# SSD units: the products of C with the states issued ahead of the multiplication that reads their PSUM bank

## The chip, the cores and the metric

The kernel runs on one core of a Trainium2 chip. The metric is the device time of one execution in microseconds (us), as the median of several runs. A core has five engines that run in parallel and meet only at semaphores: TensorE (PE, matrix products; its weight loads are shown apart as PEld), VectorE (DVE), ScalarE (ACT), GpSimd (POOL) and SyncE (SP, which here issues DMAs). Results of PE land in PSUM, which has banks of 512 float32 values for each of its 128 partitions.

## The reference, cut to what matters

One inference step of one layer of a hybrid decoder, in float32: 272 prompt rows (256 and 16 meta tokens) and 64 sample rows (8 sequences of 8 tokens), width 2048.

```
u = rmsnorm(h) @ w_in
h = h + concat[SSD(...), mLSTM(...)] @ w_out
h = h + (silu(gate) * val) @ w_down      # gate, val = split(conv(rmsnorm(h) @ w_up))
y = rmsnorm(h)
```

The change lies in the SSD part (Mamba-2, 32 heads in 2 groups, head width 64, state width 128). For each chunk of rows it computes

```
def step(S, inp):
    xc, dtc, Bc, Cc = inp
    cum = jnp.cumsum(dtc * Ag, axis=1)
    ...
    y = jnp.einsum('btsg,btsge,bsge,bsgep->btgep', CB, decay, dtc, xc)
    y = y + jnp.einsum('btgn,bgepn,btge->btgep', Cc, S, jnp.exp(cum))
    tail = jnp.exp(cum[:, -1:] - cum) * dtc
    S = S * jnp.exp(cum[:, -1])[..., None, None] + jnp.einsum('bsgn,bsge,bsgep->bgepn', Bc, tail, xc)
```

The second term of y is what matters here: the product of C with the state S, times exp(cum). The prompt has chunks of 16, 128 and 128 rows, so it needs C with two states (after 16 and after 144 rows). Each sample sequence has a carried state of its own.

## The kernel before, in words

Activations stand transposed: 128 features on the partitions, the rows in the free dimension (columns 0 to 255 prompt, 256 to 319 samples, then the meta tokens). The weights stream through in blocks of 128 x 1024 (8 tiles of 128 x 128) by DMA on SP's queue. Each weight block is split into a high and a low half of a shorter format (`hi` by ACT, `lo` by DVE), and each tile takes three matrix products (lines 203 to 205). The raw blocks and both halves have three buffers each, and the split runs two blocks ahead of PE.

The stages are: the input projection with the mLSTM heads, the input projection with the SSD units, the output projection, the up projection with a convolution, the down projection, and the final norm. In the SSD stage there are 16 units, each with two heads (128 features) and two projections (x and z) of 16 tiles each, so four weight blocks. A unit's own work is a Python generator (`unit`, line 781). `gemm` calls `tick` after each 8 tiles, and each tick lets every living generator take one step, up to its next `yield`. A unit's steps so spread over some two following units: convolution, decay matrices, transposes of xs (`transpose3`), E = exp(cum) (lines 828 to 830), the reads of the samples' states and the products within a chunk (lines 832 to 858), and the step of the change (lines 861 to 876). At one point of time PE therefore issues, after the last tile of one projection: unit j's step of the change, and right behind it unit j+1's transposes of xs (line 458), and then the next projection's tiles.

The step of the change works in one PSUM bank, `pe`, which the profile names nm after its tag (two banks of that tag):

- `turned` (line 483) transposes `ys`, the samples' reads of their states, into columns 256 to 383 of the bank (line 488);
- `es`, the 64 sample columns of E, is multiplied by it on DVE (line 863, the profile's line 72);
- two products on PE of C (`cf`) with the states S1 and S2 write columns 0 to 127 and 128 to 255 (lines 864 and 865);
- the prompt's 256 columns of E are multiplied by these on DVE (line 866);
- two state updates on PE (line 870) write two banks of the tag st, and DVE adds them to the states (line 872); E is added to y (line 873), POOL multiplies by the gate (line 874).

Two engines are kept from being in one PSUM bank at a time: where an instruction writes a bank, it waits for the earlier readers on other engines of any column of it. PE and SP issue in the order of the program (line 86); the order of DVE, ACT and POOL is chosen at build time by a planner with costs of its own, so a DVE instruction that is later in the program can come first if the planner expects its inputs sooner. Helpers record their own line in the profile: products line 69, DVE's two-operand operations line 72.

Of the kernel before, what the change touches and what calls it, by code (L numbers as in the profile page):

```python
# [13 lines left out]
ADD, SUB, MUL, MAX, MIN = ALU.add, ALU.subtract, ALU.mult, ALU.max, ALU.min  # L14
# [35 lines left out]
def hymba_kernel(ctx, tc, cst, xT, w0, w1, wo, wu, wd, shist, s0, c0n, fhist,  # L50
# [4 lines left out]
    def tl(pool, shape, dt=F32, tag=None, **kw):  # L55
        uid[0] += 1
        return pool.tile(shape, dt, tag=tag, name=f"{tag}_{uid[0]}", **kw)
# [10 lines left out]
    def mm(out, lhsT, rhs, start=True, stop=True):  # L68
        nc.tensor.matmul(out, lhsT, rhs, start=start, stop=stop)  # L69

    def tt(out, a, b, op):
        nc.vector.tensor_tensor(out, a, b, op=op)  # L72
# [10 lines left out]
    def bank(pool, n, tag="g"):  # L83
        return tl(pool, [P, 512], tag=tag)[:, :n]
# [6 lines left out]
    def C(name, i=0, n=None):  # L91
        o, w = _CST[name]
        return cs[:, o + i:o + (w if n is None else i + n)]
# [167 lines left out]
    a = []  # L261
# [26 lines left out]
    with ExitStack() as pa:  # L288
# [194 lines left out]
        def turned(ys, pst=None):  # L483

            n = ys.shape[1] // P
            pst = tl(pt, [P, 4, P], tag="tr") if pst is None else pst
            for i in range(n):
                nc.tensor.transpose(pst[:, i, :], ys[:, i * P:(i + 1) * P], C("ident"))
            v = pst[:, :n, :].rearrange("p i (b u t) -> p i u b t", u=4, t=TS)
            return [v[:, i, :2] for i in range(n)]  # L490
# [16 lines left out]
        def sb(t):  # L507
            return t.rearrange("p (s b t) -> p s b t", s=2, t=TS)
# [200 lines left out]
        with tc.tile_pool(name="sd", reuse_waits="tile", bufs=1) as sd:  # L709
# [71 lines left out]
            def unit(j, gc, pad, ps, zz):  # L781
# [50 lines left out]
                ys = tl(sd, [P, P], tag="ys")  # L832
# [27 lines left out]
                yield  # L860
                es = sb(E[:, NP:ND])
                pe = bank(pm, 512, "nm")
                tt(es, es, turned(ys, pe[:, 256:384].rearrange("p (a b) -> p a b", a=1))[0], MUL)
                mm(pe[:, 0:128], S1, cf[:, 0:128])
                mm(pe[:, 128:256], S2, cf[:, 128:256])
                tt(E[:, :256], E[:, :256], pe[:, :256], MUL)
                pps = [tl(pm, [P, 512], tag="st").rearrange("p (a b) -> p a b", a=4) for _ in range(2)]
                for i, pp in enumerate(pps):
                    rows = slice(32 * i, 32 * i + 32)
# [11 lines left out]
            for g in range(2):  # L881
                bc, gc = [], []
                pad = padded(16 + g)
                start(conv(pad, (early.pop(1 + g) if 1 + g in early else inproj(1 + g)), 16 + g, bc))
                pad = padded(18 + g)
                ps = (early.pop(3 + g) if 3 + g in early else inproj(3 + g))
                start(conv(pad, ps, 18 + g, bc, tl(sd, [P, T], tag="cf")))
                start(group(bc, gc))
                for j in range(8 * g, 8 * g + 8):
                    zz = []  # L890
                    pad = padded(j)
                    start(unit(j, gc, pad, (early.pop(5 + 2 * j) if 5 + 2 * j in early else inproj(5 + 2 * j)), zz))
                    start(zgate(inproj(6 + 2 * j, NQ), zz))
# [250 lines left out]
```

## Time and profile before

| | |
|---|---|
| median of 3 runs | 1961.93 us (1961.51 to 1962.8) |
| profiled execution | 1962.04 us |
| its span (first to last instruction) | 1960.3 us |
| granted TensorE clock, mean | 0.997 |
| PE busy | 1929.2 us (98%) |
| DVE busy | 1240.5 us (63%) |
| ACT busy | 856.3 us (44%) |
| POOL busy | 381.5 us (19%) |
| mean DMA rate | 163 GB/s |
| SSD units in the span | from about 455 to 800 us |

A line of the view in order of time has the start, the length, the engine, the line of the code, the operation, the tile written and the tiles read; xN says that N records were merged, and brackets hold the idle time of the engine ahead of it and what ended it. A line of the waits has the engine and tile that waited, for whom, the sum in us, the number of times and the longest. Ends of matrix products are modelled.

### The profile page before, as it was taken

How to read it: one execution, taken by the hardware profiler on the slowest of the kernel's cores; microseconds unless marked ns; L12 is line 12 of the kernel's file. 1: busy time of each engine (PE TensorE's matmuls, PEld its weight loads, DVE VectorE, ACT ScalarE, POOL GpSimd, SP SyncE). 2: the span in 40 equal slices, each digit the busy share in tenths (PEclk: the TensorE clock that was granted, in tenths of full speed). 3: DMA queues.
4: the chain of work that ended last, by engine and by line, in shares of the span. 5: the costliest groups of instructions: out<-in, count | busy, mean ns of one | idle time of the engine just before them, and what ended most of it. 6: DMA issues, size and time to landing. Idle time of an engine off the chain costs nothing.

```text
span 1960.3 us, 33606 instructions
## 1 busy us (share of the span) xinstructions
PE 1929.2 (98%) x13302; PEld 1891.2 (96%) x13302; DVE 1240.5 (63%) x2064; ACT 856.3 (44%) x1301; POOL 381.5 (19%) x721
## 2 busy tenths in 40 slices
PE   9999999999999999999999999999999999999997
PEld 8999999999989998999999999999999999999997
DVE  7877676777888788655547666655555556333344
ACT  6355555555444455433334444443334435333332
POOL 1211111212434343211112111111111110111111
PEclk9999999999999999999999999999999999999998
DMA  7545555546554655455554444444444444555553
GB/s 228 178 150 191 175 174 179 193 156 204 185 182 162 199 178 180 150 161 157 163 165 145 154 146 149 153 153 150 148 153 151 152 147 150 148 150 151 152 148 113
DMA packets 94221, 319.68 MB, mean 163 GB/s; under 512 B 10680, under 2 KB 19440, under 8 KB 92016
## 3 DMA queue, kind: packets, MB, share of 16 engines
q1 hardware_dynamic: 93744, 317.26, 50.7%
q8 instruction: 104, 1.70, 0.4%
q10 hardware_dynamic: 320, 0.28, 0.1%
q14 instruction: 53, 0.43, 0.1%
HBM read 294.80 MB, written 22.70 MB: 162 GB/s over the span
## 4 chain that ended last, share of the span: by engine, by line
PE 94%; DVE 3%; DMA 1%; issue 1%; ACT 1%; SPq 0%; DVEq 0%; ACTq 0%
PE g L69 87%; PE st L69 3%; PE nm L69 2%; DMA rowB<-scr_m 1%; PE tr L458 1%; DVE lo L72 1%; DVE blk L78 0%; DVE yb L72 0%; ACT hi L81 0%; DVE blk L72 0%; DMA raw<-in_w 0%; DVE co L78 0%; DVE pad L72 0%; DVE blk L552 0%; PE tr L69 0%
## 5 line engine op out<-in xcount | busy, mean ns | idle before, releaser
L69 PE MATMUL g<-blk,hi 128*128 128x322 f32 (+2 forms) x6240 | 1429.5, 313 | 0.0
L69 PEld LDWEIGHTS g<-blk,hi 128*128 128x128 f32 x6240 | 1054.1, 189 | 5.5 <-issue 4.8
L72 DVE TENSOR_TENSOR lo<-raw,hi 128x1024 fp32r<-128x1024 f32 (+3 forms) x509 | 652.6, 1282 | 464.6 <-ACT hi L81 459.5
L69 PE MATMUL g<-blk,lo 128*128 128x322 f32 (+2 forms) x2992 | 930.8, 311 | 0.0
L81 ACT ACTIVATE hi<-raw 128x1024 fp32r<-128x1024 f32 (+2 forms) x507 | 527.6, 1041 | 760.7 <-PE g L69 521.4
L69 PEld LDWEIGHTS g<-blk,lo 128*128 128x128 f32 x2992 | 563.8, 188 | 0.0
L69 PE MATMUL g<-ah,hi 128*128 128x322 f32 (+1 forms) x832 | 259.6, 312 | 0.0
L69 PE MATMUL g<-ah,lo 128*128 128x322 f32 (+1 forms) x832 | 259.5, 312 | 0.0
L69 PE MATMUL g<-al,hi 128*128 128x322 f32 (+1 forms) x832 | 258.8, 311 | 0.0
L69 PEld LDWEIGHTS g<-ah,hi 128*128 128x128 f32 x832 | 158.2, 190 | 0.1
L69 PEld LDWEIGHTS g<-al,hi 128*128 128x128 f32 x832 | 157.3, 189 | 0.1
L69 PEld LDWEIGHTS g<-ah,lo 128*128 128x128 f32 x832 | 157.1, 189 | 0.0
L72 DVE TENSOR_TENSOR fpad<-g,R 128x256 f32<-128x256 f32 (+2 forms) x264 | 54.6, 263 | 95.2 <-PE g L69 95.1
L235 POOL TENSOR_TENSOR blk<-h 128x322 f32<-128x322 f32 (+1 forms) x28 | 31.0, 1107 | 400.1 <-DVE h L72 231.8
L78 DVE SCALAR_TENSOR_TENSOR fcv<-fpad,fc,fcv 128x336 f32<-128x336 f32 x176 | 99.4, 567 | 3.9 <-ACT fcv L81 0.8
L976 POOL COPY fo<-fpad 128x2 f32<-128x2 f32 x88 | 17.5, 199 | 338.7 <-DVE fpad L72 338.6
L81 ACT ACTIVATE blk<-blk 128x322 fp32r<-128x322 f32 (+6 forms) x118 | 50.4, 450 | 51.7 <-DVE blk L78 20.9
L75 POOL TENSOR_TENSOR blk<-fsg,fcv 128x256 f32<-128x256 f32 x88 | 46.6, 553 | 112.2 <-PE g L69 60.9
L81 ACT ACTIVATE fcv<-fpad,fc 128x336 f32<-128x336 f32 x88 | 57.2, 652 | 0.1
L81 ACT ACTIVATE fsg<-fcv 128x336 f32<-128x336 f32 x44 | 21.3, 484 | 73.1 <-DVE fcv L78 73.1
L236 POOL TENSOR_TENSOR acc<-acc,blk 128x322 f32<-128x322 f32 (+2 forms) x46 | 51.8, 1126 | 2.5
L72 DVE TENSOR_TENSOR blk<-blk,blk 128x322 fp32r<-128x322 f32 (+3 forms) x76 | 38.9, 522 | 18.4 <-ACT blk L81 18.0
(212 smaller groups left out, 1340.0 us busy)
## 6 DMA issues: line engine op xcount, KB each, us to landing
raw<-in_wu SPq DMA_DIRECT2D x176, 512.0 KB, 3.7
raw<-in_w SPq DMA_DIRECT2D x164, 512.0 KB, 4.1
raw<-in_wd SPq DMA_DIRECT2D x80, 512.0 KB, 3.6
raw<-in_wo SPq DMA_DIRECT2D x64, 512.0 KB, 4.1
out_c_o<-co SPq DMA_DIRECT2D x8, 1156.5 KB, 7.4
out_ssd_o<-so SPq DMA_DIRECT2D x16, 576.0 KB, 3.7
C<-in_c0n SPq DMA_DIRECT2D x8, 1028.0 KB, 6.6
S<-in_s SPq DMA_DIRECT2D x16, 512.0 KB, 4.9
```

Source lines behind the costliest of these rows:

```text
L69: nc.tensor.matmul(out, lhsT, rhs, start=start, stop=stop)
L72: nc.vector.tensor_tensor(out, a, b, op=op)
L75: nc.gpsimd.tensor_tensor(out, a, b, op=op)
L78: nc.vector.scalar_tensor_tensor(out, a, s, b, op0=op0, op1=op1)
L81: nc.scalar.activation(out, a, f, **kw)
L235: eng.tensor_tensor(q, x, x, op=MUL)
L236: eng.tensor_tensor(self.acc[eng], self.acc[eng], q, op=ADD)
L458: nc.tensor.transpose(pst[:n, c, :], src[:, o:o + n], C("ident"))
L976: nc.gpsimd.tensor_copy(fo[:, li, 0:2], pad[:, 256:258])
```

## The change

The DVE multiplication of the samples' columns by the transposed reads is moved from between the transposes and the products of C with the states to behind the multiplication of the prompt's columns. Operands, tiles and banks stay as they are.

```diff
                 es = sb(E[:, NP:ND])
                 pe = bank(pm, 512, "nm")
-                tt(es, es, turned(ys, pe[:, 256:384].rearrange("p (a b) -> p a b", a=1))[0], MUL)
+                yt = turned(ys, pe[:, 256:384].rearrange("p (a b) -> p a b", a=1))[0]
                 mm(pe[:, 0:128], S1, cf[:, 0:128])
                 mm(pe[:, 128:256], S2, cf[:, 128:256])
                 tt(E[:, :256], E[:, :256], pe[:, :256], MUL)
+                tt(es, es, yt, MUL)
                 pps = [tl(pm, [P, 512], tag="st").rearrange("p (a b) -> p a b", a=4) for _ in range(2)]
```

## The prediction

> **What bounds the kernel now.** I read the totals of the page first, then the chain that ended last, then what TensorE (PE) waited for, then the order of time around the lines that the change touches.
>
> ```profile
> span 1960.3 us, 33606 instructions
> PE 1929.2 (98%) x13302; PEld 1891.2 (96%) x13302; DVE 1240.5 (63%) x2064; ACT 856.3 (44%) x1301; POOL 381.5 (19%) x721
> PE 94%; DVE 3%; DMA 1%; issue 1%; ACT 1%; SPq 0%; DVEq 0%; ACTq 0%
> ```
>
> PE is the bound: 1929.2 of 1960.3 us, and 94% of the chain. Nothing that other engines do counts unless PE stands for it. So the next view is the list of what PE waited for in the whole span, its four largest entries:
>
> ```profile
> PE nm L69 <- DVE pad L72: 9.0, 14, 0.7
> PE tr L458 <- DVE blk L72: 2.0, 3, 1.1
> PE nm L69 <- DVE lo L72: 1.7, 2, 1.1
> PE nm L69 <- DVE E L72: 1.5, 2, 1.1
> ```
>
> The columns are total us, times, longest. The first and the fourth are 14 + 2 = 16 waits, 10.5 us in all, one for each of the 16 SSD units: tile nm is written late because VectorE (DVE) has not finished with it. The view in order of time of one unit, and of the next one's start, shows what they are:
>
> ```profile
> 526.52 0.27 PE L488 MATMUL nm<-cs,ys 128*128 128x128 f32 x1
> 526.72 0.42 DVE L72 TENSOR_TENSOR pad<-g,R 128x256 f32<-128x256 f32 x1 [0.86 <-PE g L69]
> 527.06 0.21 DVE L72 TENSOR_TENSOR E<-E,nm 128x64 f32<-128x64 f32 x1
> 527.18 0.36 DVE L72 TENSOR_TENSOR pad<-g,R 128x64 f32<-128x64 f32 x3
> 527.41 0.68 PE L69 MATMUL nm<-cf,S 128*128 128x128 f32 x4 [0.63 <-DVE pad L72]
> 528.02 1.13 PE L69 MATMUL st<-xm,bt 32*128 32x512 f32 x4
> 529.08 0.55 PE L458 MATMUL tr<-cs,blk 128*128 128x128 f32 x3
> 529.39 0.54 PE L69 MATMUL g<-blk,hi 128*128 128x322 f32 x2
> 546.06 0.27 PE L488 MATMUL nm<-cs,ys 128*128 128x128 f32 x1
> ```
>
> At 526.52 PE transposes the samples' reads (line 863, through line 488) into columns 256 to 383 of bank pe. DVE is first busy with the 256-wide padding of the next unit (526.72), then multiplies E's 64 sample columns by the transposed reads (527.06 to 527.27). Only then, at 527.41, do the products of C with S1 and S2 begin (lines 864 and 865). They read none of what DVE made; they write columns 0 to 255 of the bank that DVE was reading. The trace puts the wait down to the padding, but the small padding at 527.18 feeds nothing in nm: the releaser is the E multiplication, whose end is 0.14 us ahead of the products.
>
> **The change part by part.** It removes, adds and resizes no instruction. On PE, whose order is the program's, the sequence stays transpose, two products (four records), two state updates, the next unit's transposes. What moves is one DVE instruction, the 64-wide multiplication (0.21 us), from ahead of the products to behind the 256-wide one. No DMA moves, so SP's and POOL's queues keep their order.
>
> *What goes.* The products no longer wait for DVE. From a transpose's start to the products' start:
>
> ```profile
> 487.35 0.27 PE L488 MATMUL nm<-cs,ys 128*128 128x128 f32 x1
> 488.31 0.68 PE L69 MATMUL nm<-cf,S 128*128 128x128 f32 x4 [0.69 <-DVE pad L72]
> 757.44 0.27 PE L488 MATMUL nm<-cs,ys 128*128 128x128 f32 x1
> 758.33 0.68 PE L69 MATMUL nm<-cf,S 128*128 128x128 f32 x4 [0.63 <-DVE pad L72]
> 776.72 0.27 PE L488 MATMUL nm<-cs,ys 128*128 128x128 f32 x1
> 778.08 0.68 PE L69 MATMUL nm<-cf,S 128*128 128x128 f32 x4 [1.08 <-DVE E L72]
> 796.49 0.27 PE L488 MATMUL nm<-cs,ys 128*128 128x128 f32 x1
> 797.17 0.68 PE L69 MATMUL nm<-cf,S 128*128 128x128 f32 x4 [0.41 <-DVE E L72]
> ```
>
> These are the first (0.96) and the fourteenth (0.89) of the ordinary units, and the last two (1.36, where DVE was behind with other work, and 0.68, where no padding stood ahead). Of the fourteen, three show 0.96, four 0.90 and seven 0.89: 2.88 + 3.60 + 6.23 = 12.71. With 1.36 and 0.68 the sixteen make 14.75 us.
>
> *What stays of it.* The transpose takes its own time in the stream, which the trace doesn't show in this place without a wait. Nearest rows: the three transposes at 529.08 are followed by g at 529.39, 0.31 / 3 = 0.10 us each; the four product records at 527.41 are followed by st at 528.02, 0.61 / 4 = 0.15 each. I take 0.15, since the products' weights have the products' own form and must be loaded in that step: 16 x 0.15 = 2.40. Saved: 14.75 - 2.40 = 12.35 us. With 0.10 it would be 13.15. The other end is the idle time that the trace itself charges, 10.5, which starts at the modelled end of the transpose's record (0.27 after its start). A record's length is not its place in a stream: at 529.08 three transposes fit into 0.31.
>
> The Trainium skill, in "TensorE: Matmul & The Clock Gate" (Single matmul latency and step 5, NX overlap), has a lone matmul last (398 + N) / 2.4 ns but successive ones start every N / 2.4: the drain lies under the next fill. For N = 128 that is 166 ns hidden; as an estimate from that page 16 x 0.166 = 2.7 on top of the idle time's 10.5 gives 13.2 saved. The transposes at 529.08 agree in kind: 0.10 apart, records 0.27 long.
>
> *The moved multiplication.* DVE now does the 64-wide one behind the 256-wide one. Its 0.21 us is the same work; the paddings come about 0.15 earlier for it. Behind it in program order stand the state additions, the addition to y and, through them, POOL's gating and ACT's E of the next unit. None of this is on the chain unless it makes PE wait later. So the question is what PE needs next, and how late it may come:
>
> ```profile
> 527.65 1.23 DVE L72 TENSOR_TENSOR lo<-raw,hi 128x1024 fp32r<-128x1024 f32 x1
> 530.85 0.61 DVE L813 TENSOR_TENSOR xp<-tr,colA 128x256 f32<-128x256 f32 x2
> 532.83 0.90 POOL L813 TENSOR_TENSOR xw<-xp,colA 128x256 f32<-128x256 f32 x1
> 534.18 1.76 DVE L72 TENSOR_TENSOR lo<-raw,hi 128x1024 fp32r<-128x1024 f32 x1
> 534.82 2.02 POOL L75 TENSOR_TENSOR xm<-xw,cs 64x512 f32<-64x512 f32 x1
> 538.26 0.61 PE L69 MATMUL st<-xw,bt 128*128 128x128 f32 x4
> 538.87 7.37 PE g L69 x48
> 540.81 0.46 DVE L78 SCALAR_TENSOR_TENSOR S<-S,dec,st 128x64 f32<-128x64 f32 x2
> 541.19 0.46 DVE L78 SCALAR_TENSOR_TENSOR so<-S,dec,st 128x64 f32<-128x64 f32 x2
> 541.58 0.70 DVE L78 SCALAR_TENSOR_TENSOR blk<-th,cv 128x256 f32<-128x256 f32 x4
> 546.96 0.68 PE L69 MATMUL nm<-cf,S 128*128 128x128 f32 x4 [0.63 <-DVE pad L72]
> ```
>
> (The row of 538.87 is from the chain.) The next products need S2, done at 541.27, and would start at 546.06 + 0.15 = 546.21: 4.9 us to spare. The state updates behind them need both "st" banks, the later one free at 541.65, against 546.82: 5.2 us. They also need xm, ready at 536.84. The transposes of the next xs need the four pieces of 541.58, done by 542.28, about 6 us before. The xw of 532.83 ends at 533.73; its first reader at 538.26 would come 0.74 earlier: 3.8 us. The weight halves run on a ring of three: the lo ending at 528.88 belongs to the block from 538.87 on, the one ending at 535.94 to the second half of that block, 3.7 later, more than 6 us ahead. All are larger than the 0.74 us that the unit becomes shorter, so no stall comes back in this place, and what PE gains in one unit it keeps.
>
> DVE's own load is the cover for all of these:
>
> ```profile
> 555.00:575.00 20.00, 19.38 (x147) 17.79 (x146) 16.80 (x33) 9.59 (x19) 8.74 (x11) 1.00 0.55 179
> ```
>
> Columns: length, busy us of PE, PEld, DVE, ACT, POOL, then granted clock, DMA share, GB/s. DVE is busy 84%. A unit is 546.06 - 526.52 = 19.54 us, of which DVE works 16.4; at 18.80 us it would be 87% busy, DMA 57% where it is 55% now. The clock is at 1.00 already and has nothing to give or to lose by 0.7 us less standing. From 798 us to the end PE waits once, so the shift reaches the end:
>
> ```profile
> PE g L69 <- DVE R L72: 0.2, 1, 0.2
> ```
>
> *The sum.* The profiled execution took 1962.04 us, its span 1960.3; the median of the runs is 1961.93, 0.11 lower. 1962.04 - 12.35 = 1949.7, and from the median 1949.6. That is 0.63% less; about 0.2% (3.9 us) is what a measurement of this kernel can tell from no change.
>
> **The rivals.**
>
> *The wait moves instead of going.* PE could meet its next DVE dependence, the "st" banks or the next xs, at the same point and stand as long. For: all the instructions behind the products depend on DVE work of the unit before. Against: the slack of 4.9 to 6 us worked out above. DVE would have to come some 5.5 us later than now. Time: 1961.9. Chance 4%.
>
> *Only part is kept.* DVE's order is chosen by a planner and not by the program, so the move can reshuffle paddings, lo halves and E's multiplications, and the last two units, where DVE is behind, can stand again. If the gain per unit fell to half, 16 x 0.37 = 5.9 saved: 1956. Chance 7%. Speaks against it: lo has over 6 us to spare.
>
> *Slower, by DVE standing at the head of its queue.* If the planner puts the 256-wide multiplication ahead of the paddings, DVE waits there for PE's products, 0.15 + 0.68 = 0.8 us after the last g, and with the state additions ahead too, 1.06 more. DVE then has 16.4 us of work and this standing in a unit of 18.80: up to 2.4 us it is free, beyond it each us lengthens the unit by one. The change would be a loss only from 19.54 - 16.4 = 3.1 us on; at 3.5 us the unit takes 19.9, 16 x 0.36 = 5.8 us more: 1967.7. The two items come to 1.9, below both points. Chance 5%.
>
> **How the numbers follow.** The likeliest case, the stall gone for good, has 84%; its own range runs from 13.15 saved (1948.8) to 10.5 saved (1951.4), and 0.8 wider at the low end, since the last two units and the rows' reading may give a little more. The whole range, 1948 to 1953, takes in the milder half of the partial case. Faster by over 0.2%: 84% and most of the partial case, 90%; within it 4% and a rest of 1%: 5%; slower 5%.
>
> **What would show it.** Right: the two entries of PE waiting for nm gone from the waits; from a transpose's start to the products' 0.10 to 0.15 us instead of 0.89; PE's busy time within a few us of 1929 and its idle time some 10 us less; a unit of about 18.8 us; the 64-wide E multiplication behind the 256-wide one on DVE. Wrong: a new entry of PE waiting for DVE at st, tr or g in this stage; products that start 0.3 us or more after the transposes; units shorter but a later stage longer because the planner ordered DVE, ACT or POOL differently there.

## The result and the profile after

The changed kernel takes 1948.09 us as the median of four runs (1947.21 to 1949.64), the kernel before, timed beside it, 1962.32 (1961.51 to 1962.8). The ratio is 0.9924, 95% interval 0.9911 to 0.9936: 0.76% faster, and a ratio so applied to the 1961.93 of before gives 1947.0. The direction and the mechanism were forecast; the size was 12.35 us and came out at 14 to 15.

The profiled execution took 1947.21 us, its span is 14.9 us shorter than that of before. First the page's lines, then PE's waits, its four largest entries (total us, times, longest):

```profile
span 1945.4 us, 33603 instructions
PE 1924.6 (99%) x13302; PEld 1890.9 (97%) x13302; DVE 1244.0 (64%) x2064; ACT 856.6 (44%) x1301; POOL 403.2 (21%) x721
```

```profile
PE nm L69 <- DVE lo L72: 2.2, 2, 1.6
PE tr L458 <- DVE blk L72: 1.7, 3, 0.8
PE g L69 <- POOL R L98: 1.2, 1, 1.2
PE nm L69 <- ACT hi L81: 0.9, 1, 0.9
```

The 9.0 and the 1.5 us for nm are gone; what is left is, in all but 0.2 us, from before 455 us, the start and the mLSTM stage. The busy times of the SSD stage, before and then after, say the same (columns: stretch, length, busy us of PE, PEld, DVE, ACT, POOL, granted clock, DMA share, GB/s): PE stood 10.47 us before and none after.

```profile
455.00:798.00 343.00, 332.53 (x2481) 307.80 (x2482) 286.12 (x566) 172.46 (x335) 135.07 (x165) 1.00 0.55 179
```

```profile
455.00:784.00 329.00, 329.00 (x2484) 308.20 (x2482) 289.66 (x569) 171.69 (x335) 154.16 (x168) 1.00 0.60 186
```

The order of time of the second unit of the changed kernel, PE and DVE:

```profile
506.70 0.27 PE L488 MATMUL nm<-cs,ys 128*128 128x128 f32 x1
506.80 0.61 PE L69 MATMUL nm<-cf,S 128*128 128x128 f32 x4
506.89 0.56 DVE L72 TENSOR_TENSOR pad<-g,R 128x256 f32<-128x256 f32 x2 [0.87 <-PE g L69]
507.34 1.13 PE L69 MATMUL st<-xm,bt 32*128 32x512 f32 x4
507.45 0.55 DVE L72 TENSOR_TENSOR E<-E,nm 128x256 f32<-128x256 f32 x2
508.04 0.49 DVE L72 TENSOR_TENSOR blk<-blk,E 128x320 f32<-128x320 f32 x1
508.40 0.55 PE L458 MATMUL tr<-cs,blk 128*128 128x128 f32 x3
508.56 1.29 DVE L72 TENSOR_TENSOR so<-S,st 128x512 f32<-128x512 f32 x2
510.57 1.21 DVE L72 TENSOR_TENSOR lo<-raw,hi 128x1024 fp32r<-128x1024 f32 x1
525.38 0.27 PE L488 MATMUL nm<-cs,ys 128*128 128x128 f32 x1
```

From transpose to products 0.10 us (0.89 before), from the products to the state updates 0.54 (0.61 before), a unit 525.38 - 506.70 = 18.68 (19.54 before). DVE's order changed more than the diff says: both multiplications of E now stand right behind two pieces of the padding, and the addition to y (`blk<-blk,E`) ahead of the lo half, which came first before.

### The profile page after: what moved, and what is told of

It is laid out like the page before. It is cut to its first block, busy times and chain, and to the rows that moved or that the text cites. A ratio compares the mean times of both kernels' runs of the same rounds, so it can differ in the third digit from the quotient of the medians.

```text
span 1945.4 us, 33603 instructions
## 1 busy us (share of the span) xinstructions
PE 1924.6 (99%) x13302; PEld 1890.9 (97%) x13302; DVE 1244.0 (64%) x2064; ACT 856.6 (44%) x1301; POOL 403.2 (21%) x721
## 4 chain that ended last, share of the span: by engine, by line
PE 95%; DVE 2%; DMA 2%; ACT 1%; issue 0%; SPq 0%; DVEq 0%; ACTq 0%
PE g L69 88%; PE st L69 3%; PE nm L69 2%; DMA rowB<-scr_m 1%; PE tr L458 1%; DVE lo L72 0%; DVE yb L72 0%; DMA raw<-in_w 0%; DVE co L78 0%; ACT hi L81 0%; ACT blk L81 0%; DVE blk L552 0%; PE tr L69 0%; DVE blk L72 0%; DVE Rs L1035 0%
## 5 line engine op out<-in xcount | busy, mean ns | idle before, releaser
L236 POOL TENSOR_TENSOR acc<-acc,blk 128x322 f32<-128x322 f32 (+2 forms) x46 | 70.1, 1524 | 3.5
```

The lines of the kernel that those rows point to most:

```text
L236: eng.tensor_tensor(self.acc[eng], self.acc[eng], q, op=ADD)
```

## The experiments

**The changed kernel again,** beside the three that follow.

> The changed kernel once more, timed beside the others. Theory (a whole stall per unit went: from the transpose's start to the state updates 1.50 us before, 0.64 after in an ordinary unit, 14.3 us over 16 units): 14.3 us less than before, between 13 and 15.5. Rival (the 14.9 us of the single comparison of spans hold more than the units, for instance a start or an up projection that runs faster in the changed kernel): 15 us or more again, with a part of it outside the units in the same place.

Measured: 1947.66 us (1946.42 to 1952.42) against 1962.55; ratio 0.9929 (0.9917 to 0.9942): 13.9 us less by the ratio, 14.9 by the medians, both within the forecast 13 to 15.5. Its profiled execution is the slowest of its runs, 1952.42 us, 5.2 slower than that of the first comparison. It shows where runs differ. Its first transpose of a unit is at 490.3 us and its last at 785.8, so the 15 steps take 295.5 us, and 783.51 - 488.02 = 295.49 in the first comparison. The units agree; the surplus lies ahead of them (2.3 us) and behind (2.9). Ahead, PE waits for DVE at the start of the program, and the clock granted right behind this wait is 0.50 for some 3 us. The wait is as long in the first comparison, 1.59 us in both, and there the clock stays at 1.00; the repeat has one more of 0.49 just ahead of it. The same stretch, in the repeat and then in the first comparison:

```profile
30.00:36.00 6.00, 4.14 (x15) 3.87 (x16) 5.28 (x8) 2.19 (x4) 0.00 (x0) 0.72 0.37 115
30.00:36.00 6.00, 4.33 (x27) 3.90 (x26) 5.26 (x7) 2.27 (x4) 0.00 (x0) 1.00 0.39 126
```

Behind, the up projection differs by itself. Its gate operation has 44 records; the line gives the start of the first and the last, in before and in the changed kernel:

```profile
L81 ACT ACTIVATE fsg<-fcv x44: 466/485/488, 1038.4 to 1632.2; 128x336 f32<-128x336 f32 x44
```

```profile
L81 ACT ACTIVATE fsg<-fcv x44: 463/484/487, 1024.7 to 1617.4; 128x336 f32<-128x336 f32 x44
```

From first to last 593.8 and 592.7, and 595.4 (1027.1 to 1622.5) in the repeat, with the same instructions. So the rival was partly right for the first pair of profiles: of 14.9 us, the units hold 14.3 (below), the start gave back 0.7, and 1.3 lie behind the units, 1.1 of it in the up projection. The start belongs to the run: the first transpose comes at 488.0 in one profile of this kernel and at 490.3 in the other. For the 1.1 this isn't shown. The three profiled kernels in which PE still waits (before, and two of the experiments below) all have 593.8 in the up projection, and those without the wait have 592.7 in five profiles and 595.4 in this repeat. So this part may go with the change by a way that no run shows, or with the run.

**The transposed reads in a bank of their own,** with the order of the program as before:

```diff
-                tt(es, es, turned(ys, pe[:, 256:384].rearrange("p (a b) -> p a b", a=1))[0], MUL)
+                tt(es, es, turned(ys)[0], MUL)
```

> The order of the program is that of before, but the transposed reads go to the bank of the tag tr instead of columns 256 to 383 of pe. Theory (PE stood because DVE read the bank that the products write): no wait of PE for nm, 0.10 us from the transpose to the products, and 14.3 us less than before (13 to 15.5), as with the change itself. Rival (the gain comes of the multiplication being late in DVE's order, with E's 256 columns ahead of it): the multiplication keeps its early place here, so little or nothing is gained, 0 to 4 us. A wait of PE for tr, where the next xs needs that one bank 1.7 us after the transpose, would show as an entry there; the multiplication ends some 0.75 us after it, so none is expected.

```profile
505.56 0.27 PE L488 MATMUL tr<-cs,ys 128*128 128x128 f32 x1
505.67 0.61 PE L69 MATMUL nm<-cf,S 128*128 128x128 f32 x4
506.10 0.21 DVE L72 TENSOR_TENSOR E<-E,tr 128x64 f32<-128x64 f32 x1
506.21 1.13 PE L69 MATMUL st<-xm,bt 32*128 32x512 f32 x4
```

Measured: 1945.9 us, ratio 0.9919 (0.9906 to 0.9933), as with the change. DVE's sample multiplication keeps its early place, 0.54 us after the transpose, and runs while PE multiplies. So what cost the time was the shared bank, and the multiplication's place on DVE is worth nothing by itself. The rival falls. PE's wait for tr, which could have taken the place, isn't there in this stage.

**Both products ahead of the transpose too,** against the changed kernel.

```diff
-                yt = turned(ys, pe[:, 256:384].rearrange("p (a b) -> p a b", a=1))[0]
                 mm(pe[:, 0:128], S1, cf[:, 0:128])
                 mm(pe[:, 128:256], S2, cf[:, 128:256])
+                yt = turned(ys, pe[:, 256:384].rearrange("p (a b) -> p a b", a=1))[0]
```

> As changed, but on PE both products stand ahead of the transpose too. Theory: PE streams the same records without a wait, so the same time as the changed kernel within 1 us (14.3 less than before). Rival (the transpose's place just behind the last projection tile is what makes it cheap, 0.10 us, or the products behind a transpose are cheap): per unit 0.05 to 0.15 us more, 1 to 2.4 us in all over the changed kernel.

```profile
505.29 0.60 PE L69 MATMUL nm<-cf,S 128*128 128x128 f32 x4
505.74 0.27 PE L488 MATMUL nm<-cs,ys 128*128 128x128 f32 x1
505.94 1.13 PE L69 MATMUL st<-xm,bt 32*128 32x512 f32 x4
```

Measured: 1947.52 us, ratio 0.9925 (0.9911 to 0.9938). From the first of the five records to the state updates 0.65 us, with the transpose first 0.64: the records cost the same in either order within 0.01 us, and the rival, 0.05 to 0.15, falls. The three kernels without the wait aren't told apart by their intervals, so none of them is better than the others.

**Half of the change:** one product ahead of the sample multiplication, one behind it (the diff is against the changed kernel).

```diff
                 mm(pe[:, 0:128], S1, cf[:, 0:128])
+                tt(es, es, yt, MUL)
                 mm(pe[:, 128:256], S2, cf[:, 128:256])
                 tt(E[:, :256], E[:, :256], pe[:, :256], MUL)
-                tt(es, es, yt, MUL)
```

> Half of the change: one product ahead of the sample multiplication, one behind it. Theory (the wait's length counts, and it ends when DVE is done): the first product (0.27 us) lies under the wait, DVE still ends some 0.75 us after the transpose's start, the second product starts at 0.89, its first record is 0.07 us longer as after any wait, and the state updates start at 1.23 instead of 1.50 before: 16 x 0.27 = 4.3 us less than before, 3 to 6. Rival (a wait costs a fixed restart whatever its length): one wait per unit remains, so nothing is gained, within 1 us of before. Rival 2 (what counts is DVE's order): the multiplication is early, nothing gained.

```profile
506.99 0.27 PE L488 MATMUL nm<-cs,ys 128*128 128x128 f32 x1
507.10 0.39 PE L69 MATMUL nm<-cf,S 128*128 128x128 f32 x2
507.53 0.21 DVE L72 TENSOR_TENSOR E<-E,nm 128x64 f32<-128x64 f32 x1
507.80 0.49 PE L69 MATMUL nm<-cf,S 128*128 128x128 f32 x2 [0.31 <-DVE E L72]
508.21 1.13 PE L69 MATMUL st<-xm,bt 32*128 32x512 f32 x4
```

Measured: 1958.9 us against 1962.55, ratio 0.9981 (0.9972 to 0.9989), 3.7 us less; forecast 4.3, 3 to 6. DVE is done at 507.74 and the second product begins 0.06 later: the wait ends with DVE, and the product put under it is free. Both rivals, which gave nothing, fall. The state updates start 1.22 us after the transpose, 1.23 forecast, but this hit is in part luck: the second product starts at 0.81 and not at 0.89, and takes 0.41 until the next instruction where 0.34 was forecast and half of 0.54 is 0.27. The fifteenth unit gains nothing: its updates start 2.15 after the transpose, 1.97 before.

**The wait lengthened,** in the kernel before; `dum` is a tile of its own that nothing reads, here and below.

```diff
-                tt(es, es, turned(ys, pe[:, 256:384].rearrange("p (a b) -> p a b", a=1))[0], MUL)
+                yt = turned(ys, pe[:, 256:384].rearrange("p (a b) -> p a b", a=1))[0]
+                tt(es, es, yt, MUL)
+                tt(sb(dum), sb(C("ones", 0, 64)), yt, MUL)
```

> The kernel before with the stall lengthened: DVE reads the transposed samples a second time (64 columns into a tile that nothing uses, some 0.2 us) right behind the multiplication and ahead of the products. Theory (PE stands exactly as long as DVE is in the bank): the products start 0.13 to 0.21 us later, 1.03 to 1.10 after the transpose's start, and the kernel is 16 x 0.13 to 0.21 = 2.1 to 3.4 us slower than before. Rival (a wait costs a fixed amount): same as before within 1 us.

```profile
527.89 0.27 PE L488 MATMUL nm<-cs,ys 128*128 128x128 f32 x1
528.92 0.68 PE L69 MATMUL nm<-cf,S 128*128 128x128 f32 x4 [0.76 <-DVE pad L72]
779.70 0.27 PE L488 MATMUL nm<-cs,ys 128*128 128x128 f32 x1
781.19 0.68 PE L69 MATMUL nm<-cf,S 128*128 128x128 f32 x4 [1.22 <-DVE dum L72]
```

Measured: 1964.62 us against 1962.54, ratio 1.0012 (1.0003 to 1.0021), 2.1 us more, at the lower edge of the 2.1 to 3.4. The interval is 0.6 to 4.1 us, so the time alone hardly shuts out the rival, which had at most 1 us. The trace does: the products start 1.03 after the transpose where it was 0.89, and over the sixteen units this wait makes 16.9 us, 14.75 before. PE stands as long as DVE is in the bank. The profiled run holds one thing more: in the fifteenth unit, where DVE is behind, the products start 1.49 after the transpose, and the granted clock falls right behind it:

```profile
779.00:785.00 6.00, 4.78 (x24) 3.63 (x23) 5.96 (x14) 2.52 (x5) 0.22 (x1) 0.82 0.51 149
785.00:789.00 4.00, 4.00 (x25) 4.00 (x24) 3.58 (x7) 2.71 (x6) 3.92 (x5) 0.84 0.48 193
```

In stretches of 2 us from 781 on the clock is 0.97, 0.50, 0.67 and 1.00, so the low part is some 3 us long. That unit took 801.20 - 779.70 = 21.50 us, against 19.77 in the kernel before, whose 1.36 in the same place left the clock at 1.00. The length of the wait doesn't decide it alone: with one product ahead, PE stood idle there for 1.24 us, 1.22 here, and kept its clock:

```profile
774.85 0.49 PE L69 MATMUL nm<-cf,S 128*128 128x128 f32 x2 [1.24 <-DVE E L72]
773.00:779.00 6.00, 4.76 (x30) 3.69 (x30) 5.78 (x14) 2.46 (x5) 0.75 (x1) 1.00 0.59 181
```

**DVE's cover used up.** The changed kernel with one and with four more 1024-wide DVE operations per unit:

```diff
+                so8 = so[:, 1:9, :].rearrange("p a b -> p (a b)")
+                for _ in range(1):        # 4 in the second
+                    tt(dum, so8, so8, MUL)
                 tt(y[:, :ND], y[:, :ND], E, ADD)
```

> The changed kernel with one 1024-wide DVE operation more per unit (about 1.2 us, into a tile that nothing uses, behind the state additions). It tests the cover: DVE is free about 2.2 of the 18.68 us of a unit. Theory: 1.2 us of the 2.2 are used up, PE gets no new wait, the same time as the changed kernel within 2 us. Rival (DVE's order leaves little of the free time in usable places): some wait of PE for lo or tr appears and the kernel loses 5 us or more of the 14.

> The same with four such operations per unit, about 4.9 us. Theory: 2.2 us are free, 2.7 over, so DVE becomes the bound of the units: 16 x 2.7 = 43 us slower than the changed kernel, 30 to 60, with PE waiting for lo. Rival (waits of DVE for ACT and PE are not usable, or the operations slow down others): more than 60. Rival 2 (buffers' slack of 6 us takes it): under 15.

Busy times from 500 to 760 us, for the changed kernel, with one and with four operations (columns as above):

```profile
500.00:760.00 260.00, 260.00 (x1962) 242.38 (x1961) 229.59 (x448) 132.59 (x262) 129.17 (x137) 1.00 0.61 188
```

```profile
500.00:760.00 260.00, 260.00 (x1962) 242.38 (x1961) 229.47 (x461) 127.63 (x261) 119.41 (x138) 1.00 0.60 188
```

```profile
500.00:760.00 260.00, 237.39 (x1678) 220.37 (x1677) 247.04 (x432) 112.14 (x222) 114.59 (x122) 0.94 0.49 161
```

One operation: 1947.48 us, ratio 0.9924 (0.9909 to 0.9939), the time of the changed kernel, and PE never stands in this stretch. Four: 2001.98 us, ratio 1.0201 (1.0187 to 1.0215), 54 us above the changed kernel; forecast 43, 30 to 60. DVE is 95% busy there, and PE waits 24.5 us for it in nine places, the largest entry:

```profile
PE g L69 <- DVE lo L72: 24.5, 9, 3.5
```

One operation of 1.28 us fits and four don't, as forecast; where between them the cover ends wasn't tried. With four, the time is in the range but not made up as the sum had it. From the first unit's transpose to the last's it takes 345.2 us, 49.7 more than in the changed kernel: PE is idle for 29.7, where the changed kernel has no idle time, and the other 20 go with a granted clock of 0.94 over these 345 us (an estimate from the two: 0.06 x 345 = 21).

## Why the prediction was right, and where it was wrong

*The stall and its cause* were right: one wait per unit of PE for DVE in the bank, behind the padding and the sample multiplication. The run with a bank of its own shows that it is the bank; the half change and the lengthened wait show that PE waits as long as DVE takes.

*The sum* was too small. From the transpose to the state updates the sixteen units took 14.75 + 16 x 0.61 = 24.5 us before and 16 x 0.64 = 10.2 after: 14.3 us. That agrees with the transposes and state updates themselves: the first transpose at 487.35 and the last state updates at 797.78 before, 488.02 and 784.16 after, 310.43 - 296.14 = 14.29. Against the 12.35 of the prediction 1.9 us are missing, in two terms: the transpose's place, which was taken too long, and the products, whose own gain was put at nothing.

The step "I take 0.15" for the transpose's place in the stream failed: it is 0.10 to 0.11. Of the two rows put side by side I took the wrong one as the nearest: the three transposes at 529.08, the same operation, had the 0.10. That is 16 x 0.045 = 0.7 us. With 0.105 the rows give 14.75 - 1.68 = 13.07 for this part. The estimate of 13.2 from the Trainium skill's "TensorE: Matmul & The Clock Gate" (Single matmul latency), whose formula is for bf16 products while these are float32, is near it: the trace agrees with the page's overlap, and not with the idle time's 10.5.

The second term was missing altogether: the sum took the products' own length as the same with and without the wait. The form rows of these products, before and then after (shortest, median, longest record in ns), show that it isn't:

```profile
L69 PE MATMUL nm<-cf,S x64: 275/275/348, 488.3 to 797.6; 128*128 128x128 f32 x64
```

```profile
L69 PE MATMUL nm<-cf,S x64: 272/275/275, 488.1 to 784.0; 128*128 128x128 f32 x64
```

The longest record, 0.35 us, is the first behind a wait, 0.07 longer than the others (at 507.86 in the kernel before), and so it takes 0.61 to the state updates and not 0.54. Sixteen of them make 1.1 us, and 0.7 + 1.1 = 1.8 of the 1.9. An idle column counts neither this nor the overlapped end of a record.

*The range* was too narrow at its low end by the same terms: 14.3 saved is 1947.6, and the ratio's 1947.0 lies 1.0 under 1948.0. The 0.6 us between these two is within the ratio's interval. The range also left out what one and the same kernel differs by from run to run, 1946.4 to 1952.4 in the repeat.

*The cover* was right. No stall came back at st, tr or g; DVE at 88% (290 of 329 us) left enough, and one more operation per unit still fitted. That DVE stands at the head of its queue, the rival for a loss, did not come up, although the planner put E's 256 columns ahead of most of the padding: the row of 507.45 has no idle time ahead of it. Four more operations show what the loss would have looked like. The wait that moves and the part that is lost did not come either. POOL's busy time in the SSD stage rose, to 154 us of 329 from 135 of 343, but PE never waits for it there.

*What would show it*: all the signs named as right are there, with a unit of 18.68 for the 18.8. The sign against it, a later stage that is longer, could have been misread: the up projection differs by 2.8 us between two profiles of the changed kernel.

## What to carry to other kernels

Where PE writes columns of a PSUM bank that another engine is still reading, look for an order, or a bank, in which nothing PE needs stands behind that read; either took off the whole stall here. Price a stall from the start of the instruction ahead of it to the start of the one two steps behind it, and take off what these steps take where nothing waits; here the idle column gave 10.5 us for what was worth 14.3. Compare a stage between the same two instructions of two profiles, and not spans, when a part of a per cent is asked.

## What the runs showed of the hardware that was not expected

DVE's busy time wasn't a fixed amount of work here. With one operation more per unit, 13 of them with 16.6 us in 260, DVE was busy for as long as without (229.5 and 229.6 us). The lo halves had become shorter, from 1759 to 1434 ns each in the mean, and POOL's accumulations from 2586 to 1678, while POOL's xw rose from 886 to 1521. That the two engines' operations lay across each other differently fits this; it wasn't tested by itself. The same 1024-wide subtraction took 1.21 us where POOL was idle, and 2.67 in the changed kernel where it lay across POOL's 1.94 us multiplication of S; elsewhere there it took 1.21 and POOL's accumulation beside it 2.67.

```profile
L72 DVE TENSOR_TENSOR lo<-raw,hi 128x1024 fp32r<-128x1024 f32 x57 | 100.3, 1759 | 17.1 <-ACT hi L81 17.1
```

```profile
L72 DVE TENSOR_TENSOR lo<-raw,hi 128x1024 fp32r<-128x1024 f32 x57 | 81.7, 1434 | 24.6 <-ACT hi L81 24.6
```

And a wait of PE of little over one us can be followed by some 3 us at half the granted clock. It came behind 1.22 us of idle time in the run with the lengthened wait, and behind 1.59 at the start of the repeat; it did not come behind 1.24 with one product ahead, nor behind the same 1.59 at the start of the first comparison. So the length of one wait doesn't tell it, and what does stays open.
